# Expert weights in DRAM: from one matrix for each expert to blocks of two experts and 128 rows

## The chip, the cores and the metric

The kernel runs on one core of one Trainium2 chip. The metric is the device time of one execution in microseconds (us), the median of several executions.

## The reference, cut to what matters

Two layers follow each other. Each has a token mixer (two kinds of attention and a short convolution) and then a mixture of experts in which each of 16 experts picks 64 of the 512 tokens:

```
N_EXPERTS = 16; EXPERT_FF = 1024; D_MODEL = 1024      # all float32
x = x + einsum(mixed, w_out)                          # end of the mixer
xs   = x[idx]                                         # 64 tokens of each expert
hid  = silu(einsum('becd,edf->becf', xs, w_gate)) * einsum('becd,edf->becf', xs, w_up)
ys   = einsum('becf,efd->becd', hid, w_down) * gate
x    = x + zeros_like(x).at[bidx, idx].add(ys)
```

The three expert weights (`w_gate`, `w_up`, `w_down`) have the shape (2 layers, 16 experts, 1024, 1024), 4 MB for each expert and matrix. All 403 MB of them are read from device memory once per execution.

## The kernel before, in words

The tokens stay on the chip. A layer is `mixer()` and then `moe()`. The change touches `moe()` alone, and there only the loads of expert weights.

`moe()` works on 8 pairs of experts, one after the other. Both experts of a pair are multiplied at the same time: their 64 tokens each make the two column halves of TensorE's weights. For a pair the order is gate (8 chunks of 128 rows, contracted one after the other into the accumulators `G`), up (8 chunks, into `U`), activation and transposes, down (8 chunks, into `Y`), and then the scatter of the results to the token rows and the gather of the next pair's tokens. TensorE's matmuls run in exactly this program order (`PEo`).

A chunk is one call of `wload` (line 888): one transfer of 1 MB, 128 partitions by 2 experts by 1024 floats, into the next of 18 slots (`wslot`). All these loads are issued by SP, in program order, on one queue. SP issues a load when TensorE has read the chunk that was in its slot 18 loads earlier; each load also has one of eight semaphores in turn (DMAHW0 to DMAHW7 in the rows below), and waits for the load that had it before. `expert_mm` (line 915) takes a chunk with four matmuls (two halves of 512 columns by two experts), 8 instructions in the trace, since one float32 matmul is two instructions there.

The last pair's down projection is written apart (lines 1024 to 1036), because its two column halves `n` are finished one after the other: 16 transfers of 512 KB (line 1029), two for each step `kp` of 256 rows, each of pieces of 512 floats. After half `n` comes its scatter (`scatter_rows`), and in the last layer its output transfers. So the last loads of a layer stand directly ahead of its end.

`layouts()` runs on the host ahead of the kernel and arranges the inputs in device memory; it is not part of the time.

Of the kernel before, what the change touches and what calls it, by code (L numbers as in the profile page):

```python
# [18 lines left out]
L = 2  # L19
# [11 lines left out]
NE = 16  # L31
FF = 1024
CAP = 2 * S // NE
KC = D // 128
# [25 lines left out]
def token_of(j, p):  # L60
    return (p // CB) * GW + CB * j + p % CB


def constants():
    c = np.zeros((128, NCON), np.float32)
    c[:, _C["ident"][0]:_C["ident"][1]] = np.eye(128, dtype=np.float32)
    c[:, _C["iota"][0]:_C["iota"][1]] = np.arange(1, CAP + 1, dtype=np.float32)[None]
    c[:, _C["iotap"][0]] = (np.arange(128) % CAP + 1).astype(np.float32)
    inv = (np.float32(10000.0) ** (-np.arange(HALF, dtype=np.float32) / np.float32(HALF))).astype(np.float32)
    for j in range(NJ):  # L70
        t = token_of(j, np.arange(128)).astype(np.float32)
        ang = (t[:, None] * inv[None, :]).astype(np.float32).astype(np.float64)
        c[:, _C["cos"][0] + j * HALF:_C["cos"][0] + (j + 1) * HALF] = np.cos(ang)
        c[:, _C["sin"][0] + j * HALF:_C["sin"][0] + (j + 1) * HALF] = np.sin(ang)
    off = _C["mask"][0]
    for j, blocks in ((0, (0, 1)), (1, (0, 1, 2)), (3, (2, 3))):
        for b in blocks:
            q = CB * j + np.arange(128) % CB
            k = CB * b + np.arange(128) % CB
            st = np.clip(q - WW // 2, 0, GW - WW)[:, None]  # L80
            ok = (k[None] >= st) & (k[None] < st + WW)
            c[:, off:off + CB] = np.where(ok, 0.0, NEG)[:, :CB]
            off += CB
    c[:, _C["fold"][0]:_C["fold"][1]] = np.arange(128)[:, None] % 32 == np.arange(NE)[None, :]
    a, b = np.arange(128)[:, None], np.arange(128)[None, :]
    before = [a // CB < b // CB, a // CB == b // CB, (a // CB == b // CB) & (a < b)]
    return np.concatenate([c] + before, axis=1).astype(np.float32)
# [6 lines left out]
def build(tc, x_in, pp_in, con_in, gm_in, rpb_in, w_in, w_uq, w_ukv, w_out, w_gate, w_up, w_down, out,  # L94
# [3 lines left out]
    PE, ACT, DVE, POOL, SP = nc.tensor, nc.scalar, nc.vector, nc.gpsimd, nc.sync  # L98
# [6 lines left out]
    def tmp():  # L105
        return w2.tile([128, 512], F32, name="tmp", tag="tmp")

    def tmpr(name):
        return w2.tile([128, 512], F32R, name=name, tag="tmp")
# [700 lines left out]
    def moe(l, M, PSUM, pp, ctx2):  # L810
# [18 lines left out]
        for i in range(CAP // 8):  # L829
            src = work if i else p32[0:32, 0:256]  # L830
# [51 lines left out]
        def wslot():  # L882
            wi[0] += 1
            return wslots[(wi[0] - 1) % NSLOT]

        def wload(src, e0, k):
            t_ = wslot()
            SP.dma_start(t_, src[l, e0:e0 + 2, k * 128:(k + 1) * 128, :].rearrange("e p c -> p e c"))
            return t_

        def onehot(p):
# [75 lines left out]
        for p in range(NE // 2):  # L967
            e0 = 2 * p
            G = [acc(), acc()]
            if p:  # L970
                gate = gates(og2, e0)
                expert_mm(G, xs, w_gate, e0)
            else:
                gather(og2, 0, 1)
                for k in range(KC):
                    if k + 1 < KC:
                        gather(og2, k + 1, 1)
                    expert_mm(G, xs, w_gate, e0, range(k, k + 1))
                gate = gates(og2, e0)
                pt = wk()  # L980
                for j in range(NJ):
                    PEo.transpose(pt[0:NE, j * 128:(j + 1) * 128], slotn[:, j, :], ident)
                ACT.copy(slotT, pt[0:NE, :])
            if p < last:
                og2 = onehot(p + 1)
            U = [acc(), acc()]
            expert_mm(U, xs, w_up, e0)

            pb = wk()
            sel = st.tile([NE, 2, CAP], BF16, name="sel", tag="sel", bufs=2)  # L990
            POOL.tensor_copy(sel, ident[0:NE, e0:e0 + 2, None].to_broadcast([NE, 2, CAP]))  # L991
            PEo.matmul(pb, sel.rearrange("p e s -> p (e s)"), slotT, start=True, stop=True)
            hids = []
            for n in range(2):
                hid = tmp()
                ACT.activation(hid, G[n], AF.Silu)  # L996
                DVE.tensor_tensor(hid, U[n], hid, op=OP.mult)  # L997
                hids.append(hid)

            if p < last:  # L1000
                gather(og2, 0, 1)
            for n in range(2):
                pt = wk()
                for k in range(4):
                    PEo.transpose(pt[:, k * 128:(k + 1) * 128], hids[n][:, k * 128:(k + 1) * 128], ident)
                ACT.copy(hT[:, 4 * n:4 * n + 4, :], pt.rearrange("p (k s) -> p k s", k=4))  # L1006
            osc = tmpr("osc")
            DVE.tensor_scalar(osc, pb, C("iotap"), None, op0=OP.is_equal)
            Y = [acc(), acc()]
            if p < last:  # L1010
                gather(og2, 1, 1)
                expert_mm(Y, hs, w_down, e0)
                ys = [parts(Y, gate, 0), parts(Y, gate, 1)]
                gather(og2, 2)
                for s_ in range(4):
                    scatter(ys[s_], osc, s_)
                    if s_ < 2:
                        ys.append(parts(Y, gate, s_ + 2))
                    if s_ in (1, 2):
                        gather(og2, 2 * s_ + 2)  # L1020
                continue

            tc.keep_in_program_order(ACT.preload_act_table_set("natural_log_exp_and_others"))
            for n in range(2):
                for kp in range(KC // 2):
                    t_ = wslot() if l == layers - 1 else wslots[(4, 5, 0, 1, 2, 3)[(4 * n + kp) % 6]]
                    t_ = t_.rearrange("p a (b c) -> p a b c", b=2)
                    for e in range(2):
                        SP.dma_start(t_[:, :, e, :], w_down[l, e0 + e, kp * 256:(kp + 1) * 256, n * 512:(n + 1) * 512]
                                     .rearrange("(k p) c -> p k c", p=128))  # L1030
                    for kk in range(2):
                        k = 2 * kp + kk
                        for e in range(2):
                            PEo.matmul(Y[n][e * 64:(e + 1) * 64, :], hs(k, e), t_[:, kk, e, :], start=k == 0,
                                       stop=k == KC - 1)
                scatter_rows(Y, osc, gate, n)
# [6 lines left out]
def layouts(x, norm_mix, w_in, q_norm_a, k_norm_a, rpb, cq_norm, w_uq, ckv_norm, w_ukv, q_norm_b, k_norm_b,  # L1043
            conv_w, out_norm, w_out, norm_ffn, w_router, b_router, w_gate, w_up, w_down):

    def cols(a):
        return np.ascontiguousarray(a.reshape(-1, 128).T)

    pps = np.zeros((L, 128, NP), np.float32)
    for l in range(L):  # L1050
        def put(name, a):
            pps[l][:, _P[name][0]:_P[name][1]] = a
        put("gffn", cols(norm_ffn[l]))
        put("gout", cols(out_norm[l]))
        put("gqa", np.concatenate([q_norm_a[l]] * 2)[:, None])
        put("gka", np.concatenate([k_norm_a[l]] * 2)[:, None])
        put("gcq", cols(cq_norm[l]))
        put("gckv", cols(ckv_norm[l]))
        put("gqb", np.concatenate([q_norm_b[l, :DH], np.ones(DH, np.float32)])[:, None])
        put("gkb", np.concatenate([k_norm_b[l, :DH], np.ones(DH, np.float32)])[:, None])  # L1060
        put("convw", conv_w[l].reshape(3, 2, 128).transpose(2, 1, 0).reshape(128, 6))
        put("brt", np.broadcast_to(b_router[l], (128, NE)))
        put("gqr", np.broadcast_to(q_norm_b[l, DH:], (128, ROPE)))
        put("gkr", np.broadcast_to(k_norm_b[l, DH:], (128, ROPE)))
        put("wrt", w_router[l].reshape(KC, 128, NE).transpose(1, 0, 2).reshape(128, KC * NE))
    xp = x.reshape(8, NJ, CB, D).transpose(1, 0, 2, 3).reshape(NJ, 128, D)
    rp = np.pad(rpb, ((0, 0), (0, 0), (0, 0), (16, 16)))
    rp = np.stack([rp[..., 15 - c:63 - c] for c in range(CB)], axis=1).reshape(L, CB, NH, 15 * 48)
    return {"x": xp, "pp": pps, "con": constants(), "norm_mix": norm_mix, "rpb": rp, "w_in": w_in, "w_uq": w_uq, "w_ukv": w_ukv,
            "w_out": w_out, "w_gate": w_gate, "w_up": w_up, "w_down": w_down}  # L1070


_ORDER = ("x", "pp", "con", "norm_mix", "rpb", "w_in", "w_uq", "w_ukv", "w_out", "w_gate", "w_up", "w_down")
# [19 lines left out]
```

## Time and profile before

| | |
|---|---|
| median of 3 runs | 1555.66 us (1555.24 to 1555.86) |
| the profiled execution's own time | 1556.42 us |
| its span, first to last instruction | 1554.6 us |
| TensorE busy | 1484.8 us, 96% of the span |
| bytes read from device memory | 438.33 MB |
| transfers of 1 MB of expert weights | 368 (128 gate, 128 up, 112 down) |
| transfers of 512 KB of expert weights | 32 |

The profiled execution is 0.76 us above the median, and its span is 1.82 us shorter than its time. TensorE is busy nearly throughout, and from about 345 to 765 us and from about 1118 to 1540 us (the two `moe()` stages) the 16 DMA engines are busy throughout as well, so the page alone does not say which of the two sets the pace there.

### The profile page before, as it was taken

What the parts mean: (1) busy time and instruction counts of PE and PEld (TensorE: products, weight loads), DVE (VectorE), ACT (ScalarE), POOL (GpSimd) and SP (SyncE); (2) the same over time, 40 slices, a digit from 0 to 9 for tenths busy, and PEclk for the clock granted to TensorE, in tenths of its full rate; (3) what the DMA queues carried; (4) which work ended last, traced back from release to release, by engine and by line L of the source; (5) the groups of instructions that cost most, each with busy time, mean ns of one, the idle gap of its engine ahead of it and who ended that gap; (6) DMA issues with size and microseconds to landing.
All of it is one profiled execution on the core that took longest, in us unless ns stands there. A gap on an engine that the chain in (4) does not pass through costs nothing. (4 is left out here: it accounts for less than half of the span.)

```text
span 1554.6 us, 20383 instructions
## 1 busy us (share of the span) xinstructions
PE 1484.8 (96%) x8028; PEld 853.0 (55%) x8030; DVE 536.0 (34%) x1220; ACT 388.6 (25%) x969; POOL 232.2 (15%) x336
## 2 busy tenths in 40 slices
PE   7999999899999999899889999998999999999897
PEld 6877766645445534434278776665455355345342
DVE  5475456612122202212164644665122022122022
ACT  6465553300000000000164655542000000000001
POOL 4642350300000000000046314402000000000000
PEclk8999999999999999999999999999999999999999
DMA  5312123979999999999932112157999999999997
GB/s 168 87 45 68 48 82 124 362 286 410 409 409 409 409 409 409 409 409 409 354 100 71 49 54 74 56 218 285 370 409 409 409 409 409 409 409 409 409 409 283
DMA packets 138463, 441.76 MB, mean 284 GB/s; under 512 B 8832, under 2 KB 31360, under 8 KB 138368
## 3 DMA queue, kind: packets, MB, share of 16 engines
q1 hardware_dynamic: 136000, 437.06, 73.1%
q10 hardware_dynamic: 2368, 3.41, 0.7%
q8 instruction: 63, 1.03, 0.3%
q14 instruction: 32, 0.26, 0.0%
HBM read 438.33 MB, written 2.10 MB: 283 GB/s over the span
## 5 line engine op out<-in xcount | busy, mean ns | idle before, releaser
L158 PE MATMUL acc<-w,fmix 128*64 128x512 f32 x3072 | 684.7, 596 | 28.4 <-DMA w<-in_w_up_dram 14.9
L158 PEld LDWEIGHTS acc<-w,fmix 128*64 128x64 f32 x3072 | 213.8, 137 | 462.3 <-issue 377.8
L997 DVE TENSOR_TENSOR tmp<-acc,tmp 128x512 f32<-128x512 f32 x32 | 22.1, 691 | 410.8 <-issue 382.9
L158 PEld LDWEIGHTS wk<-og,fmix 128*128 128x128 f32 x1024 | 121.0, 192 | 25.9 <-issue 22.7
L158 PE MATMUL wk<-og,fmix 128*128 128x128 f32 x1024 | 132.2, 279 | 0.7 <-DVE og L893 0.7
L991 POOL CAST sel<-con 16x128 bf16<-16x128 f32 x16 | 4.9, 312 | 784.9 <-PE wk L158 778.6
L331 POOL TENSOR_TENSOR wring<-fraw,wring 128x384 fp32r<-128x384 f32 (+1 forms) x88 | 91.2, 1045 | 139.4 <-ACT wring L330 134.0
L996 ACT ACTIVATE tmp<-acc 128x512 f32<-128x512 f32 x32 | 18.9, 596 | 327.3 <-PE acc L158 327.3
L934 DVE SCALAR_TENSOR_TENSOR ys<-acc,stat,ys 128x256 fp32r<-128x256 f32 x56 | 26.8, 479 | 210.3 <-ACT ys L933 210.3
L933 ACT ACTIVATE ys<-acc,stat 128x256 fp32r<-128x256 f32 x56 | 26.5, 474 | 254.5 <-PE acc L158 203.3
L1006 ACT COPY fmix<-wk 128x512 f32<-128x512 f32 x32 | 17.4, 588 | 257.4 <-PE wk L161 257.4
L167 PE MATMUL prj<-wring,hn 128*128 128x384 f32 (+1 forms) x224 | 81.3, 363 | 0.2 <-DVE hn L310 0.2
L166 PE MATMUL prj<-wring,hn 128*128 128x384 f32 (+1 forms) x224 | 80.6, 361 | 0.4 <-ACT wring L330 0.4
L168 PE MATMUL prj<-wring,hn 128*128 128x384 f32 (+1 forms) x224 | 79.8, 356 | 0.1
L947 DVE TENSOR_TENSOR x<-wk,x 128x512 f32<-128x512 f32 x112 | 72.0, 684 | 2.2
L158 PE MATMUL wk<-ys,osc 128*128 128x256 f32 x448 | 63.8, 290 | 0.0
L903 DVE TENSOR_TENSOR fmix<-wk,pp 128x128 f32<-128x128 f32 (+1 forms) x86 | 30.6, 356 | 81.5 <-PE wk L158 81.5
L158 PEld LDWEIGHTS wk<-ys,osc 128*128 128x128 f32 x448 | 56.2, 191 | 0.0
L330 ACT CAST wring<-fraw 128x384 fp32r<-128x384 f32 (+1 forms) x88 | 44.4, 513 | 39.6 <-PE prj L167 15.6
L167 PEld LDWEIGHTS prj<-wring,hn 128*128 128x128 f32 x224 | 43.5, 194 | 5.6 <-issue 4.0
L168 PEld LDWEIGHTS prj<-wring,hn 128*128 128x128 f32 x224 | 43.3, 193 | 5.3 <-issue 3.7
L166 PEld LDWEIGHTS prj<-wring,hn 128*128 128x128 f32 x224 | 43.5, 194 | 4.8 <-issue 3.0
(272 smaller groups left out, 1992.7 us busy)
## 6 DMA issues: line engine op xcount, KB each, us to landing
w<-in_w_gate_dram SPq DMA_DIRECT2D x128, 1024.0 KB, 18.4
w<-in_w_up_dram SPq DMA_DIRECT2D x128, 1024.0 KB, 18.5
w<-in_w_down_dram SPq DMA_DIRECT2D x112, 1024.0 KB, 18.4
w<-in_w_down_dram SPq DMA_DIRECT2D x32, 512.0 KB, 10.8
fraw<-in_w_in_dram SPq DMA_DIRECT2D x24, 384.0 KB, 3.2
fraw<-in_w_out_dram SPq DMA_DIRECT2D x16, 512.0 KB, 3.5
fraw<-in_w_in_dram SPq DMA_DIRECT2D x48, 128.0 KB, 2.5
fmix<-in_rpb_dram ACTq DMA_DIRECT2D x16, 144.0 KB, 3.4
```

The costliest lines, as they stand in the source:

```text
L158: return tc.keep_in_program_order(PE.matmul(*a, **k))
L166: PE.matmul(ps, ah, bh, start=first, stop=False)
L167: PE.matmul(ps, al, bh, start=False, stop=False)
L168: PE.matmul(ps, ah, bl, start=False, stop=last)
L330: ACT.copy(hi, raw[:, kk, :])
L331: POOL.tensor_tensor(lo, raw[:, kk, :], f(hi), op=OP.subtract)
L903: DVE.tensor_tensor(xsT[:, k0:k0 + nk, :], pg[:, 0:nk * 128].rearrange("p (k s) -> p k s", k=nk), P("gffn")[:, k0:k0 + nk, None].to_broadc ...
L933: ACT.activation(ys[:, 0:256], yq, AF.Copy, scale=gate)
L934: DVE.scalar_tensor_tensor(ys[:, 256:512], yq, gate, f(ys[:, 0:256]), op0=OP.mult, op1=OP.subtract)
L947: DVE.tensor_tensor(xv, po.rearrange("p (j c) -> p j c", j=2), xv, op=OP.add)
L996: ACT.activation(hid, G[n], AF.Silu)
L997: DVE.tensor_tensor(hid, U[n], hid, op=OP.mult)
```

## The change

On the host, `layouts()` rearranges each expert matrix from (layer, expert, row, column) to (layer, pair, chunk of 128 rows, row in the chunk, expert of the pair, column). In device memory a chunk of a pair is then one contiguous block of 1 MB, and the 8 KB that one partition receives lie in one run; before, they were two runs of 4 KB, 4 MB apart.

`wload` reads that block as it lies. In the last pair's down projection the two transfers of a step are cut in another way: before, one transfer brought both chunks (`k`) of one expert; now one brings both experts of one chunk. Their pieces stay 512 floats (2 KB) long, and bytes and count of transfers stay what they were.

```
 def wload(src, e0, k):
     t_ = wslot()
-    SP.dma_start(t_, src[l, e0:e0 + 2, k * 128:(k + 1) * 128, :].rearrange("e p c -> p e c"))
+    SP.dma_start(t_, src[l, e0 // 2, k])
     return t_
...
     t_ = t_.rearrange("p a (b c) -> p a b c", b=2)
-    for e in range(2):
-        SP.dma_start(t_[:, :, e, :], w_down[l, e0 + e, kp * 256:(kp + 1) * 256, n * 512:(n + 1) * 512]
-                     .rearrange("(k p) c -> p k c", p=128))
+    for kk in range(2):
+        SP.dma_start(t_[:, kk], w_down[l, p, 2 * kp + kk, :, :, n * 512:(n + 1) * 512])
     for kk in range(2):
         k = 2 * kp + kk
         for e in range(2):
             PEo.matmul(Y[n][e * 64:(e + 1) * 64, :], hs(k, e), t_[:, kk, e, :], start=k == 0,
                        stop=k == KC - 1)
...
+def pairs(w):
+    return w.reshape(L, NE // 2, 2, KC, 128, FF).transpose(0, 1, 3, 4, 2, 5)
...
-        "w_out": w_out, "w_gate": w_gate, "w_up": w_up, "w_down": w_down}
+        "w_out": w_out, "w_gate": pairs(w_gate), "w_up": pairs(w_up),
+        "w_down": pairs(w_down)}
```

On SP, at the end of the last pair's up loads in the second layer, the queue before holds these rows (a row is a source line, a transfer with its target and source, and the shape of one transfer, partitions by elements):

```order
L888 DMA w_8277<-in_w_up_dram 128x2x1024
L888 DMA w_8278<-in_w_up_dram 128x2x1024
L1029 DMA w_8282<-in_w_down_dram 128x2x512 x2
L1029 DMA w_8283<-in_w_down_dram 128x2x512 x2
L1029 DMA w_8266<-in_w_down_dram 128x2x512 x2
```

The same place on SP with the change:

```order
L888 DMA w_8277<-in_w_up_dram 128x2048
L888 DMA w_8278<-in_w_up_dram 128x2048
L1029 DMA w_8282<-in_w_down_dram 128x2x512 x2
L1029 DMA w_8283<-in_w_down_dram 128x2x512 x2
L1029 DMA w_8266<-in_w_down_dram 128x2x512 x2
```

Order, slots and count of the transfers are the same; the loads of line 888 (368 of them) have become one run of 2048 floats for each partition, and the 512 KB transfers have the shape that they had.

On TensorE, the end of the second layer's last down projection (steps `kp` 2 and 3 of the second column half) stands so, with - for before and + for the change; the names in brackets are the semaphores of the transfers (DMAHW) that a matmul waits for:

```order
 L158 MATMUL acc<-w_8270,fmix 64x512 [waits DMAHW5_49]
+L158 MATMUL acc<-w_8270,fmix 64x512
 L158 MATMUL acc<-w_8270,fmix 64x512 [waits DMAHW0_49]
-L158 MATMUL acc<-w_8270,fmix 64x512 x2
+L158 MATMUL acc<-w_8270,fmix 64x512
 L158 MATMUL acc<-w_8271,fmix 64x512 [waits DMAHW2_49]
+L158 MATMUL acc<-w_8271,fmix 64x512
 L158 MATMUL acc<-w_8271,fmix 64x512 [waits DMAHW3_49]
-L158 MATMUL acc<-w_8271,fmix 64x512 x2
+L158 MATMUL acc<-w_8271,fmix 64x512
```

The second transfer of a step was waited for by the second of its four matmuls, and is now waited for by the third: two matmuls stand behind the last transfer of a half where three stood. The same holds in all 16 steps of the two layers, and nothing else moves on TensorE, VectorE, ScalarE or GpSimd.

## Rows read from the trace of the kernel before

**Rows 1.** The page: busy time of the engines; DMA in 40 slices.

```profile
PE 1484.8 (96%) x8028; PEld 853.0 (55%) x8030; DVE 536.0 (34%) x1220; ACT 388.6 (25%) x969; POOL 232.2 (15%) x336
...
GB/s 168 87 45 68 48 82 124 362 286 410 409 409 409 409 409 409 409 409 409 354 100 71 49 54 74 56 218 285 370 409 409 409 409 409 409 409 409 409 409 283
```

**Rows 2.** Stretches: busy us of each engine, clock, DMA share, GB/s.

```profile
345.00:750.00 405.00, 392.57 (x2155) 185.39 (x2153) 80.68 (x160) 29.06 (x56) 1.98 (x7) 1.00 1.03 408
1118.00:1521.00 403.00, 388.99 (x2137) 183.96 (x2133) 80.68 (x160) 29.07 (x56) 1.70 (x6) 1.00 1.03 409
1521.00:1530.00 9.00, 8.54 (x39) 3.47 (x40) 2.04 (x3) 2.46 (x3) 0.00 (x0) 1.00 1.05 387
```

**Rows 3.** What TensorE waited for: us in total, times, longest us.

```profile
PE acc L158 <- DMA w<-in_w_up_dram: 14.9, 24, 1.7
PE acc L158 <- DMA w<-in_w_down_dram: 12.9, 22, 0.7
```

**Rows 4.** Chain that ended last, second layer, in order of time: start, us, what.

```profile
1136.98 10.18 PE wk L158 x88
1147.15 27.62 PE acc L158 x128
...
1191.83 10.17 PE wk L158 x88
...
1301.51 10.17 PE wk L158 x88
...
1357.95 10.18 PE wk L158 x88
...
1419.33 10.18 PE wk L158 x88
...
1480.76 10.16 PE wk L158 x88
...
1532.12 1.95 PE acc L158 x6
...
1537.30 7.00 DMA w<-in_w_down_dram
1544.30 0.04 issue
1544.34 1.95 PE acc L158 x6
...
1550.86 0.60 DVEq L1088
```

**Rows 5.** Timeline of TensorE, last pair's up: start, us, instructions, idle before.

```profile
1512.46 1.94 PE L158 MATMUL acc<-w,fmix 128*64 128x512 f32 x8 [0.62 <-DMA w<-in_w_up_dram]
1515.02 1.94 PE L158 MATMUL acc<-w,fmix 128*64 128x512 f32 x8 [0.62 <-DMA w<-in_w_up_dram]
...
1521.28 1.94 PE L158 MATMUL acc<-w,fmix 128*64 128x512 f32 x8 [0.69 <-DMA w<-in_w_up_dram]
```

**Rows 6.** DMA packets, 1200 to 1500 us; the queue: packets, MB, share of 16 engines.

```profile
DMA packets 31780, 122.69 MB, mean 409 GB/s; under 512 B 1871, under 2 KB 1871, under 8 KB 31764
...
q1 hardware_dynamic: 31764, 122.45, 102.4%
```

**Rows 7.** The same, 1523 to 1531 us (512 KB transfers in flight).

```profile
DMA packets 1597, 3.07 MB, mean 384 GB/s; under 512 B 96, under 2 KB 96, under 8 KB 1597
...
q1 hardware_dynamic: 1597, 3.07, 104.5%
```

**Rows 8.** The same, 1236 to 1237.5 us.

```profile
q1 hardware_dynamic: 158, 0.60, 101.2%
q14 instruction: 1, 0.01, 1.3%
```

**Rows 9.** Timeline of SP: start, us, transfers issued.

```profile
1441.93 20.39 SPq L888 DMA_DIRECT2D w<-in_w_down_dram  x8
1462.41 20.35 SPq L888 DMA_DIRECT2D w<-in_w_gate_dram  x8
1482.86 18.41 SPq L888 DMA_DIRECT2D w<-in_w_up_dram  x7
```

**Rows 10.** The page: packets of the instruction queues, whole span.

```profile
q8 instruction: 63, 1.03, 0.3%
q14 instruction: 32, 0.26, 0.0%
```

## The prediction

> **What bounds the kernel now.** I read the page first: TensorE is 96% busy, and in the slices of both expert stages the DMA engines move 409 GB/s without a dip [rows 1]. Two resources are full at once, so the question is which one makes the other wait. The table of stretches puts numbers to it: from 345 to 750 us and from 1118 to 1521 us the DMA share is 1.03 at 408 and 409 GB/s, while TensorE idles for 12.4 and 14.0 us in them [rows 2]. TensorE's waits name the loads of up and down weights, 27.8 us over 46 waits [rows 3]. The chain of the second layer shows why so few. The same point of the work (the 88 instructions of scatter and gather) comes at 1136.98 and 1191.83 us: a pair takes TensorE 54.85 us. Later it comes at 1301.51, 1357.95, 1419.33 and 1480.76 us: 56.4, then 61.4 us for each pair [rows 4]. 24 loads of 1 MB (1,048,576 bytes) at 409 GB/s take 24 x 2.563 = 61.5 us. So TensorE starts a stage on slots loaded ahead, gains on the loads by 6.6 us with each pair, and from the fifth pair on goes at the pace of the loads: its chunks begin 2.56 us apart, 1.94 us of work and 0.62 us of wait [rows 5]. From about 345 and 1118 us to the last up load the transfer engines never stop, so what a transfer costs there comes back at the end of the stage, once for each transfer. SP is no limit: it issues one load after the other with no gap between them, at the pace at which they land (20.4 us for 8) [rows 9].
>
> **The 368 loads of 1 MB.** The change leaves the bytes and halves the pieces, if a run of 8 KB is moved as one packet. What does a packet cost besides its bytes? In the long stretch there are 31764 - 1871 = 29893 packets of 4 KB (122.4 MB) [rows 6]; behind the last up load, 2 KB packets alone (1501 of them, 3.07 MB) [rows 7] run at 387 GB/s [rows 2]. With 16 engines, a packet of 4096 B is spaced 4096 x 16 / 409 = 160.2 ns, one of 2048 B 2048 x 16 / 387 = 84.7 ns. A straight line through both gives 9.1 ns for a packet and 151.1 ns for 4 KB. A packet of 8 KB is then 9.1 + 302.2 = 311.3 ns, 1 MB (8 packets on each engine) 2.490 us instead of 2.563: 0.073 us less, or 421 GB/s. That is an extrapolation by one doubling. The records of the packets themselves give another price: 1.024 x 16 x 300 us / 29893 = 164 ns and 1.045 x 16 x 8 us / 1501 = 89 ns, so 2 x 89 - 164 = 14 ns a packet, and 0.11 us for a transfer. These records overlap (shares above 100%), so I take the spacing and keep 14 ns as a bound. The other bound is nothing.
>
> How many transfers count: 403 us / 2.563 = 157 in the second layer's stretch, 405 us at 408 GB/s likewise 157 in the first [rows 2]. Ahead of the stretch TensorE frees slots more slowly than they are filled, and there a faster transfer only waits. 157 x 0.073 = 11.5 us for each layer, 22.9 us in all. TensorE can take all of it: alone it would have ended the last up chunk at 1301.51 + 3 x 54.85 + 10.2 + 27.6 = 1503.9 us [rows 4], and it ended at 1521.28 + 1.94 = 1523.2 us [rows 5], so 19 us are there. With 24 x 2.490 = 59.8 us for a pair the loads still bind, and the waits remain, shorter and begun about a pair later.
>
> [...]
>
> **The 512 KB transfers at a layer's end.** Their pieces stay 2 KB, so their pace stays at 387 GB/s (1.355 us each); I cost the new addresses at nothing. But two matmuls now stand behind the last landing instead of three. Today 6 instructions take 1.95 us from the landing [rows 4], and 8 take 1.94 [rows 5], because a matmul for one expert alone takes as long as both experts side by side. Four instructions are one such pair less: a chunk in full flow is 27.62 us / 128 x 8 = 1.73 us [rows 4], half of that 0.86 us. At the layer's end this lies on the chain (landing at 1544.30, 6 instructions, scatter, output), so 0.86 us for each layer, 1.7 us in all. In the first column half the matmuls end earlier too, but the second half's last landing decides.
>
> **Other effects.** A packet of 8 KB holds an engine for 0.31 us instead of 0.16 us, so an instruction fetch on another queue can wait up to 0.15 us longer: 95 packets [rows 10], at most 14 us if each were waited for in full. TensorE's waits name no such thing today, so I cost it at nothing. The host's rearrangement lies outside the time.
>
> **Sum.** 22.9 + 1.7 = 24.6 us. The span of 1554.6 us becomes 1530.0 us; the median lies 1.06 us above the span, so 1531 us, or -1.6%.
>
> **Rivals.**
> *No wider packet, or no cost for each packet.* Nothing in the trace shows the weights' queue move a packet over 4 KB, so the 8 KB run may be cut at 4 KB. Or the fixed part belongs to the transfer, not the packet: both stretches have 16 packets on each engine for each transfer, so their rates alone cannot tell 9.1 ns a packet from 0.146 us a transfer. Then only 1.7 us come: 1554 us, within 0.2%. Against it: the recorded packets themselves are longer than in proportion (89 and 164 ns), and another queue does move packets of 8 KB (32 of 0.26 MB [rows 10]), one of them in 0.013 x 16 x 1.5 = 0.31 us beside the full load [rows 8]. [...]
> *Part of the gain.* The packet's price falls with its size, or instruction fetches take some back: 5 us for each layer instead of 11.5 gives 1544 us.
> *TensorE becomes the bound.* At 0.11 us a transfer the loads would give 157 x 0.11 = 17 us for each layer, near the 19 us that TensorE has: 1555.7 - 34 - 1.7 = 1520 us. Then a pair takes nearly 54.85 us throughout.
> *Slower.* All 16 engines now read side by side in one block of 1 MB, where each transfer spread over two blocks of 512 KB that lie 4 MB apart. If the memory serves that worse, every 1% of rate costs 314 x 0.0256 = 8.0 us, and nothing hides it, since the stretch has no slack. It shows as slower (over 0.2%, 3.1 us) from 1.7 + 3.1 = 4.8 us on, a transfer of 2.578 us. At the lowest rate that a stretch full of weights shows (387 GB/s, 2.71 us) it would be 157 x 0.147 = 23 us for each layer: 1600 us. For it: no row shows this pattern of addresses. Against: in the last pair, pieces of 2 KB out of every 4 KB run at a rate that packet size alone explains.
>
> **How the numbers follow.** A measurement of this kernel tells about 0.2% (3.1 us) from no change. Forecast (1524 to 1538 us) 0.60; part of the gain (1538 to 1552) 0.10; no gain from the packets 0.15; TensorE as the bound 0.02; slower 0.13. Faster is 0.60 + 0.10 + 0.02 = 0.72, same 0.15, slower 0.13. The range from 1523 to 1555 us leaves out the slower cases and the far end of the gain; the forecast's own range is 1524 to 1538.
>
> **What would show it.** Right: the weights' queue has about half the packets in the stretches (some 15 thousand of 8 KB in 300 us); some 421 GB/s; chunks 2.49 us apart where TensorE waits; late pairs 59.8 us; 4 instructions behind the last landing, about 1.1 us. Wrong: 409 GB/s with packets still at 4 KB (cut), or 409 GB/s with packets of 8 KB (the fixed part was the transfer's); a rate below 407 GB/s (addresses); or early pairs longer than 54.85 us, which would be a new wait that I do not see.

## The result, and the profile after

The changed kernel takes 1531.84 us (median of 4 runs, 1530.07 to 1532.34) against 1555.76 us: the ratio is 0.9844, 95% interval 0.9832 to 0.9857, so 23.9 us or 1.6% faster. The prediction was 1531 us. (A ratio is taken over executions at an undisturbed clock: one of the four of the run e4_two_transfers below took 2132.10 us at a granted clock of 0.915, against 0.964 to 0.972 in the others, so it counts in that run's median of 1958.27 us below and not in its ratio.) The profiled execution is the fastest of the four, 1530.07 us with a span of 1528.3 us, 26.3 us below the span of before.

The page of the changed kernel, the rows that answer to [rows 1], and the packets of the whole span (a packet is one piece of a transfer, as the profile records it):

```profile
PE 1478.7 (97%) x8030; PEld 855.0 (56%) x8030; DVE 537.0 (35%) x1220; ACT 388.8 (25%) x969; POOL 232.4 (15%) x336
...
GB/s 171 86 48 59 31 111 99 362 282 418 414 421 421 422 421 420 421 421 421 374 92 73 50 55 53 79 175 321 332 411 422 421 421 421 421 421 421 421 421 306
DMA packets 91359, 441.76 MB, mean 289 GB/s; under 512 B 8832, under 2 KB 31360, under 8 KB 44160
```

The same row of the kernel before:

```profile
DMA packets 138463, 441.76 MB, mean 284 GB/s; under 512 B 8832, under 2 KB 31360, under 8 KB 138368
```

The bytes are the same; the packets fell from some 138 thousand to 91 thousand, and the flat stretches stand at 421 GB/s instead of 409. The table of stretches (columns as in [rows 2]), nearly the same pieces of the program:

```profile
345.00:740.00 395.00, 390.39 (x2157) 186.65 (x2155) 80.70 (x160) 29.09 (x56) 1.99 (x7) 1.00 1.01 420
1100.00:1500.00 400.00, 395.55 (x2184) 188.72 (x2182) 82.72 (x163) 30.70 (x59) 1.70 (x6) 1.00 1.01 419
1500.00:1507.00 7.00, 6.34 (x30) 1.53 (x26) 0.00 (x0) 0.86 (x1) 0.00 (x0) 1.00 1.05 387
```

TensorE idles for 4.6 and 4.5 us in the two long stretches, where it idled for 12.4 and 14.0 us. The 2 KB packets behind the last up load (third row) run at 387 GB/s as before. TensorE's waits for weights, against the 27.8 us of [rows 3]:

```profile
PE acc L158 <- DMA w<-in_w_up_dram: 5.2, 10, 0.6
PE acc L158 <- DMA w<-in_w_down_dram: 4.9, 12, 0.6
```

The chain of the second layer now runs through loads alone late in the stage, so the pace of a pair is read from TensorE's timeline instead, at an instruction group that each pair has once (start, us):

```profile
1133.33 0.96 PE L158 MATMUL wk<-aff,og 128*128 128x16 f32 x8
...
1188.17 0.96 PE L158 MATMUL wk<-aff,og 128*128 128x16 f32 x8
...
1352.69 0.96 PE L158 MATMUL wk<-aff,og 128*128 128x16 f32 x8
...
1407.53 0.96 PE L158 MATMUL wk<-aff,og 128*128 128x16 f32 x8
...
1466.79 0.96 PE L158 MATMUL wk<-aff,og 128*128 128x16 f32 x8
```

A pair takes 54.84 us as long as the slots that were loaded ahead last, and 59.3 us in the one that waits. Before, the fifth pair was the first to slow down (56.4, then 61.4 us) [rows 4]; now it is the seventh. The chunks of the last up projection, which stand to [rows 5]:

```profile
1490.48 1.94 PE L158 MATMUL acc<-w,fmix 128*64 128x512 f32 x8 [0.26 <-DMA w<-in_w_up_dram]
1492.98 1.94 PE L158 MATMUL acc<-w,fmix 128*64 128x512 f32 x8 [0.56 <-DMA w<-in_w_up_dram]
1495.48 1.94 PE L158 MATMUL acc<-w,fmix 128*64 128x512 f32 x8 [0.57 <-DMA w<-in_w_up_dram]
```

They begin 2.50 us apart instead of 2.56, and the last one begins at 1495.48 us instead of 1521.28. The packets from 1200 to 1480 us, which answer to [rows 6]:

```profile
DMA packets 16175, 117.87 MB, mean 421 GB/s; under 512 B 1799, under 2 KB 1799, under 8 KB 1799
...
q1 hardware_dynamic: 16160, 117.65, 101.1%
```

16160 - 1799 = 14361 packets carry 117.6 MB: 8 KB each. The end of the chain in order of time (start, us, what):

```profile
1506.33 1.10 PE acc L158 x4
...
1509.53 3.35 PE wk L158 x7
1512.88 7.04 PE acc L158 x32
...
1522.08 2.60 PE wk L158 x7
```

Four instructions stand behind the first half's last landing, 1.10 us instead of 1.95.

### The profile page after: what moved, and what is told of

It reads as the page before. It is cut to its first block, busy times and chain, and to the rows that moved or that the text cites. A ratio compares the mean times of both kernels' runs of the same rounds, so it can differ in the third digit from the quotient of the medians.

```text
span 1528.3 us, 20385 instructions
## 1 busy us (share of the span) xinstructions
PE 1478.7 (97%) x8030; PEld 855.0 (56%) x8030; DVE 537.0 (35%) x1220; ACT 388.8 (25%) x969; POOL 232.4 (15%) x336
## 5 line engine op out<-in xcount | busy, mean ns | idle before, releaser
L158 PE MATMUL acc<-w,fmix 128*64 128x512 f32 x3072 | 675.2, 595 | 10.4 <-DMA w<-in_w_up_dram 5.2
```

The source lines that it names most:

```text
L158: return tc.keep_in_program_order(PE.matmul(*a, **k))
```

## The experiments

**Which part, and which property of it?** The change alters three things at once: the size of a packet, the addresses of a load (one block instead of two), and the cut of the last transfers. Three runs take them apart.

*Only the cut of the last transfers*, on the layout of before:

```
-for e in range(2):
-    SP.dma_start(t_[:, :, e, :], w_down[l, e0 + e, kp * 256:(kp + 1) * 256, n * 512:(n + 1) * 512]
-                 .rearrange("(k p) c -> p k c", p=128))
+for kk in range(2):
+    k = 2 * kp + kk
+    SP.dma_start(t_[:, kk], w_down[l, e0:e0 + 2, k * 128:(k + 1) * 128, n * 512:(n + 1) * 512]
+                 .rearrange("e p c -> p e c"))
```

> The old layout and the old 1 MB loads; only the last pair's 512 KB transfers are cut by chunk instead of by expert. Packet price (the theory of the prediction) and its rivals agree on the loads: 2.56 us for each, 409 GB/s, as before. The cut alone should bring 0.5 to 0.9 us for each layer (4 instructions behind the last landing instead of 6): 1554 to 1555 us, not to be told from before by the times; in the profile, from the last up load's landing to the end of the span 32.5 to 32.9 us instead of 33.4.

1555.23 us; ratio 0.9991, interval 0.9982 to 1.0000. The loads run as before (the stretch, then the queue from 1200 to 1480 us, of this kernel):

```profile
1118.00:1518.00 400.00, 387.88 (x2133) 183.63 (x2129) 80.70 (x160) 29.07 (x56) 1.70 (x6) 1.00 1.03 409
```

```profile
q1 hardware_dynamic: 29640, 114.28, 102.4%
```

Nearly all of the gain lies in the loads of line 888. What the cut brings is at the edge of what the times can tell, but TensorE's timeline shows it at the second layer's end (the last up chunk):

```profile
1521.13 1.94 PE L158 MATMUL acc<-w,fmix 128*64 128x512 f32 x8 [0.64 <-DMA w<-in_w_up_dram]
```

From the start of the last up chunk to the end of its span of 1554.0 us it took 32.9 us, within the 32.5 to 32.9 that were expected; before, it was 1554.6 - 1521.28 = 33.3 us [rows 5].

*The block of the change, but 4 KB packets*:

```
-    return w.reshape(L, NE // 2, 2, KC, 128, FF).transpose(0, 1, 3, 4, 2, 5)
+    w = w.reshape(L, NE // 2, 2, KC, 128, FF).transpose(0, 1, 3, 4, 2, 5)
+    return np.pad(w, ((0, 0),) * 5 + ((0, 64),))
...
-    SP.dma_start(t_, src[l, e0 // 2, k])
+    SP.dma_start(t_, src[l, e0 // 2, k, :, :, 0:FF])
```

> The changed kernel, but 256 B of padding stand behind each expert's 4 KB in device memory, so that the same block is read in packets of 4 KB; transfers, order and addresses are otherwise those of the change. Packet price: 16 packets on each engine again, 2.56 us a load, 409 GB/s, 1554 us. Rival, the addresses (one block instead of two that lie 4 MB apart) gave the gain: 2.49 us a load, about 1532 us.

1555.96 us; ratio 0.9997, interval 0.9988 to 1.0007. Its queue from 1200 to 1480 us:

```profile
DMA packets 29660, 114.51 MB, mean 409 GB/s; under 512 B 1743, under 2 KB 1743, under 8 KB 29645
```

409 GB/s: with 4 KB packets the block brings nothing.

*8 KB packets without a block* (a partition's runs 64 KB apart; the last transfers are read from the same layout):

```
-    return w.reshape(L, NE // 2, 2, KC, 128, FF).transpose(0, 1, 3, 4, 2, 5)
+    return w.reshape(L, NE // 2, 2, KC, 128, FF).transpose(0, 1, 4, 3, 2, 5)
...
-    SP.dma_start(t_, src[l, e0 // 2, k])
+    SP.dma_start(t_, src[l, e0 // 2, :, k])
...
-        SP.dma_start(t_[:, kk], w_down[l, p, 2 * kp + kk, :, :, n * 512:(n + 1) * 512])
+        SP.dma_start(t_[:, kk], w_down[l, p, :, 2 * kp + kk, :, n * 512:(n + 1) * 512])
```

> The changed kernel with packets of 8 KB, but a partition's runs lie 64 KB apart in device memory: no contiguous block for any load. Packet price: 2.49 us a load, about 421 GB/s, 1532 us, as with the change. Rival, the contiguous block gave the gain: at least 2.56 us a load, 1554 us or more.

1530.34 us; ratio 0.9834, interval 0.9817 to 0.9850. Its queue in the same stretch:

```profile
DMA packets 16174, 117.87 MB, mean 421 GB/s; under 512 B 1798, under 2 KB 1798, under 8 KB 1798
```

421 GB/s: the whole gain, from scattered addresses. At the addresses tried here the size of the run decides, not where the runs lie, and the theory of addresses falls on both sides.

**Is the price one for each packet, or one for each transfer?** The first attempt doubled the transfers of the changed kernel by halves of the partitions:

```
-    SP.dma_start(t_, src[l, e0 // 2, k])
+    for h in range(2):
+        SP.dma_start(t_[h * 64:(h + 1) * 64], src[l, e0 // 2, k, h * 64:(h + 1) * 64])
```

> The changed kernel, but each 1 MB load is two transfers of 64 partitions; packets stay at 8 KB and their number is the same, the number of transfers doubles. Packet price: 2.49 to 2.51 us for 1 MB, 1532 to 1537 us. Rival, the fixed part (0.146 us) belongs to each transfer: 2.63 us for 1 MB, which is 157 x 0.146 = 23 us more for each layer, about 1577 us.

1958.27 us; ratio 1.257, interval 1.2546 to 1.2595: slower than either theory said. Its queue from 1500 to 1700 us:

```profile
DMA packets 9517, 62.44 MB, mean 312 GB/s; under 512 B 1902, under 2 KB 1902, under 8 KB 1902
...
q1 hardware_dynamic: 9509, 62.32, 101.8%
```

9509 - 1902 = 7607 packets of 8 KB take 1.018 x 16 x 200 us / 7607 = 428 ns each, where the changed kernel has 1.011 x 16 x 280 / 14361 = 315 ns. The rate is not the same throughout: in the two stages the slices of its page go from 219 to 323 GB/s.

```profile
GB/s 154 65 54 58 66 160 220 224 282 297 293 295 309 308 306 282 307 316 308 290 57 52 62 63 50 219 230 274 294 302 320 323 312 310 284 243 238 244 295 259
```

The packets themselves have become longer, so this run does not answer the question that it was made for. The next one doubles the transfers over all 128 partitions, on the kernel before:

```
-    SP.dma_start(t_, src[l, e0:e0 + 2, k * 128:(k + 1) * 128, :].rearrange("e p c -> p e c"))
+    for e in range(2):
+        SP.dma_start(t_[:, e], src[l, e0 + e, k * 128:(k + 1) * 128, :])
```

> The kernel before, but each 1 MB load is two transfers of 512 KB over all 128 partitions, one for each expert: packets stay at 4 KB, their number is the same, the number of transfers doubles. Packet price: 2.56 us for 1 MB plus one more completion packet on each engine (the few-byte packets, some 0.01 us), 1555 to 1560 us. Rival, the fixed part (0.146 us) belongs to each transfer: 2.71 us for 1 MB, 157 x 0.146 = 23 us more for each layer, about 1602 us.

1554.46 us; ratio 0.9983, interval 0.9974 to 0.9992. The queue from 1200 to 1480 us:

```profile
DMA packets 31402, 114.50 MB, mean 409 GB/s; under 512 B 3488, under 2 KB 3488, under 8 KB 31387
...
q1 hardware_dynamic: 31387, 114.29, 102.5%
```

Twice the few-byte packets (3488), the same 409 GB/s. A transfer has no price that shows here; the price belongs to the packet. The run is even 2.7 us faster than the kernel before beside it (1557.16 us), just below the 1555 to 1560 that were expected; where that comes from was not followed up.

**Why was the split by halves so slow?**

```
-    SP.dma_start(t_, src[l, e0 // 2, k])
+    for h in range(2):
+        SP.dma_start(t_[h:128:2], src[l, e0 // 2, k, h:128:2])
```

> As e4_two_transfers (two transfers of 64 partitions for 1 MB, packets of 8 KB), but the transfers take the even and the odd partitions instead of the lower and the upper half. Theory for the slow e4: 16 engines that write into 64 neighbouring partitions get in each other's way at the on-chip memory (packets of 468 ns instead of 312 in e4); alternate partitions spread over all of it, so packets of about 312 ns, 2.5 us for 1 MB, 1532 to 1540 us. Rival, a transfer over 64 partitions is slow by itself: as e4, about 1958 us.

1532.34 us; ratio 0.9842, interval 0.9826 to 0.9859. Its queue from 1200 to 1480 us:

```profile
DMA packets 17958, 117.83 MB, mean 421 GB/s; under 512 B 3588, under 2 KB 3588, under 8 KB 3588
...
q1 hardware_dynamic: 17942, 117.60, 101.1%
```

Also two transfers of 64 partitions for 1 MB, and as fast as one: 1.011 x 16 x 280 / (17942 - 3588) = 316 ns a packet. (The 468 ns of the expectation are the spacing at a rate of 280 GB/s, 8192 x 16 / 280; the recorded length in the window shown is 428 ns.) So it is the choice of 64 neighbouring partitions that stretches packets, 428 ns against 316. The two runs differ in the source addresses as well, but e5_by_expert reads contiguous blocks of 512 KB, as the run by halves does, without a loss (409 GB/s, as the kernel before). That engines get in each other's way at the on-chip memory is the author's theory; the runs show the lengths of the packets, not what lies behind them.

**Does the line go on?** Two chunks in one transfer, runs of 16 KB, 9 slots of 2 MB (left out: the order of the slots, and the halves of slots that the first layer's last transfers get):

```
-    wslots[i] = M.tile([128, 2, FF], F32, name=f"w{i}", tag=f"w{i}")
+    wslots[i] = M.tile([128, 2, 2, FF], F32, name=f"w{i}", tag=f"w{i}")
...
+    if k % 2 == 0:
+        wcur[0] = wslot()
+        SP.dma_start(wcur[0], src[l, e0 // 2, k // 2])
+    return wcur[0][:, k % 2]
...
+    return w.reshape(L, NE // 2, 2, KC // 2, 2, 128, FF).transpose(0, 1, 3, 5, 4, 2, 6)
```

> The changed kernel with two chunks in one transfer: 2 MB, a run of 16 KB for each partition, 9 slots of 2 MB instead of 18 of 1 MB. Packet price on the same line: 9.1 + 604.4 = 613.5 ns a packet, 2.454 us for 1 MB, 427 GB/s, 157 x 0.031 = 4.9 us less for each layer; the coarser slots are freed one chunk later, which costs about 2 us for each layer: about 1526 us (1523 to 1530). Rival, a packet ends at 8 KB or has a price that grows with its size: 2.49 us for 1 MB, 1532 to 1537 us.

1531.06 us (1527.51 to 1532.57); ratio 0.9832, interval 0.9814 to 0.9849. Its queue from 1200 to 1480 us, the stretch behind the first layer's up loads, and what SP waited for there (us in total, times, longest us):

```profile
DMA packets 8211, 119.62 MB, mean 427 GB/s; under 512 B 909, under 2 KB 909, under 8 KB 909
```

```profile
735.00:755.00 20.00, 15.71 (x69) 5.52 (x67) 5.08 (x9) 3.40 (x5) 0.28 (x1) 1.00 0.96 339
```

```profile
SPq L1036 <- DMA w<-in_w_up_dram: 29.2, 3, 24.1
```

The rate is the one on the line, 427 GB/s, but the time is hardly below the change's and misses the expected 1523 to 1530 us. The last loads of the first layer (the stretch) run with gaps at 339 GB/s: they had been given slots that the last up loads still held, and SP waited up to 24.1 us for one of these.

*Runs of 4 KB in the last down projection*, on the changed kernel (left out: the load of line 1029, which reads the new blocks as they lie):

```
+    last = w_down[:, NE - 2:].reshape(L, 2, KC, 128, 2, 512).transpose(0, 4, 2, 3, 1, 5)
+    down[:, -1] = last.reshape(down[:, -1].shape)
```

> The changed kernel with the last pair's down weights laid out by column half, so that its 512 KB transfers have runs of 4 KB instead of 2 KB. Packet price: 1.28 us for each 512 KB instead of 1.355 (16 packets of 4 KB on each engine for 1 MB), so the first half's last landing comes 8 x 0.075 = 0.6 us earlier after the last up load; up to 1.2 us for each layer, 1529.5 to 1531.5 us, hardly to be told by the times, but by the landings in the trace. Rival, these loads are bound by the semaphores or the memory and not by their packets: still 1.355 us.

1531.17 us; ratio 0.9834, interval 0.9819 to 0.9848. The stretch behind its last up load:

```profile
1498.00:1506.00 8.00, 7.95 (x41) 2.81 (x37) 2.04 (x3) 2.45 (x3) 0.00 (x0) 1.00 1.03 410
```

410 GB/s where the change has 387: these loads follow their packets too. The landings show it as well, at the last up chunk of the second layer and at the matmuls behind the first half's last landing:

```profile
1497.48 1.94 PE L158 MATMUL acc<-w,fmix 128*64 128x512 f32 x8 [1.08 <-DMA w<-in_w_up_dram]
1507.73 1.08 PE L158 MATMUL acc<-w,fmix 128*64 128x512 f32 x4 [0.20 <-DMA w<-in_w_down_dram]
```

They lie 10.25 us apart, where the change has 1506.33 - 1495.48 = 10.85: the 0.6 us that were expected. The time does not tell it from the change, as was expected.

**A faster version.** The two runs that followed gave the 2 MB slots other places in memory, so that the first layer's last transfers find free slots; the second also has the 4 KB runs at the end. The changed kernel ran beside them.

```
-    for i in (2, 3, 4, 6, 7, 0, 5, 8, 1):
+    for i in (5, 6, 7, 8, 1, 2, 3, 4, 0):
...
+    t_ = wslots[(2, 3, 4, 0)[i_ // 2]][:, i_ % 2]
```

> As e6_16k (2 MB transfers, runs of 16 KB), with other slots for the first layer's last down projection. In e6_16k the last up load of the first layer landed 4.5 us earlier than with the change, but the next layer began no earlier, since the tail's first transfers waited for the slot of the last up load. Theory: with slots that are free by then the 4.5 us come through, 1531.1 - 4.5 = 1526.5 us (1525 to 1528). Rival, something else binds the first layer's end (TensorE, or the mixer's memory): 1530 to 1532 us.

> e10_16k_slots and e7_tail_4k together: 2 MB transfers with runs of 16 KB, and runs of 4 KB in the last pair's down projection. Packet price: 0.6 to 1.2 us for each layer less than e10_16k_slots, 1524 to 1526 us. Rival, the tail is TensorE's by now: as e10_16k_slots.

> The changed kernel itself beside the two others, for a comparison on one chip: 1530 to 1533 us.

1546.57 us (ratio 0.9937, interval 0.9921 to 0.9952), 1548.00 us (0.9945, 0.9932 to 0.9958) and 1532.45 us (0.9849, 0.9832 to 0.9866). Both theories for the slots were wrong. SP's timeline of the first of them, as the mixer of the second layer ends (start, us, transfers), and a wait of SP there:

```profile
1027.78 34.29 SPq L889 DMA_DIRECT2D w<-in_w_gate_dram  x4
1062.17 2.69 SPq L889 DMA_DIRECT2D w<-in_w_up_dram  x4
```

```profile
SPq L889 <- PE prj L168: 32.5, 1, 32.5
```

The first four loads took 34 us to issue and the next four followed within 3 us: the second load's slot stood in memory that the mixer used nearly to its end (SP waited 32.5 us for a matmul of the mixer), and SP, which issues in order, held all others behind it. The stage began with fewer slots filled: from 1010 to 1090 us the DMA engines moved 176 GB/s, where e6_16k has 297. The last run changes the places once more:

```
-    for i in (5, 6, 7, 8, 1, 2, 3, 4, 0):
+    for i in (1, 4, 5, 7, 8, 2, 3, 6, 0):
...
-    t_ = wslots[(2, 3, 4, 0)[i_ // 2]][:, i_ % 2]
+    t_ = wslots[(2, 3, 0, 2)[i_ // 2]][:, i_ % 2]
```

> As e8_16k_tail_4k, but the nine slots stand in memory so that the first four loads of a stage go where the mixer's buffers are released first (in e10_16k_slots the second load of each stage waited 33 us for its slot, and SP, which issues in order, held all others behind it), and the first layer's last transfers go to slots that are free by then. Theory: the prefetch is whole again and the wider packets come through, 1524 to 1527 us. Rival, the 2 MB slots cost as much as the packets bring (coarser release): 1530 to 1532 us, as e6_16k.

1523.38 us (1522.46 to 1526.26); ratio 0.9799, interval 0.9784 to 0.9814, which lies wholly below that of the change. Two stretches, and TensorE's waits for weights, of this kernel:

```profile
345.00:735.00 390.00, 387.52 (x2151) 186.75 (x2147) 80.70 (x160) 29.07 (x56) 1.98 (x7) 1.00 1.01 426
735.00:755.00 20.00, 17.14 (x79) 6.53 (x79) 5.49 (x9) 3.40 (x5) 0.28 (x1) 1.00 0.99 395
```

```profile
PE acc L158 <- DMA w<-in_w_down_dram: 5.0, 4, 1.4
PE acc L158 <- DMA w<-in_w_up_dram: 2.7, 3, 1.2
```

The tail of the first layer is full again (395 GB/s where e6_16k has 339), the long stretch is at 426 GB/s, and TensorE waits for weights 7.7 us in all. The run holds three things at once (runs of 16 KB, the places of the slots, runs of 4 KB at the end), and their shares were not taken apart.

## Why the prediction was right

*The bound.* It said that a late pair goes at the pace of the loads and that their time comes back at the end of the stage. It did: the chunks moved from 2.56 to 2.50 us apart, and the last up chunk of the second layer came 25.8 us earlier.

*The packet's price.* From 2 KB and 4 KB packets the line gave 9.1 ns a packet and 421 GB/s for 8 KB. Measured are 421 GB/s, and for 16 KB 427 GB/s, that is 16384 x 16 / 427 = 614 ns where the line has 613.5. That this is a price of the packet, not of the transfer, the place or the layout, was argued ahead and is now shown by three runs: 4 KB packets from the same block give no gain (409 GB/s), 8 KB packets from scattered runs give it all (421 GB/s), and twice the transfers cost nothing (409 GB/s). The recorded lengths, by which a packet would cost 14 ns, overstated it. The sum chose the 387 GB/s of [rows 2] for 2 KB packets; with the 384 of [rows 7] the same line gives 10.4 ns a packet and 423 GB/s, so the exact hit on 421 is in part that choice.

*How much of it reaches the end.* 22.9 us were counted for the loads. The last up chunk's 25.8 us hold that of both layers, the first layer's tail, and whatever else differs between two executions; the medians differ by 23.9 us, of which the cut of the last transfers has part. In the first layer alone, where 11.5 us were counted, the last up chunk came 752.36 - 739.15 = 13.2 us earlier in this pair of executions, and 11.9 to 12.7 us earlier in the traces of after_again, e3_pitch_64k, e7_tail_4k and e9_alternate. So the term was, if anything, a little small; it agrees with the medians within what the runs scatter. One statement was off without a cost: the waits were to begin about a pair later, and began two pairs later.

*The last transfers.* 0.86 us for each layer were counted, at the second half's last landing. The matmuls behind a last landing did shrink from 1.95 to 1.10 us, but neither layer went the way that the prediction gave.

In the first layer the size was right and the path was not. The last up chunk and the second column half, the kernel before (two rows) and then the changed one (two rows):

```profile
752.36 1.94 PE L158 MATMUL acc<-w,fmix 128*64 128x512 f32 x8 [0.61 <-DMA w<-in_w_up_dram]
769.05 7.09 PE L158 MATMUL acc<-w,fmix 128*64 128x512 f32 x32
739.15 1.94 PE L158 MATMUL acc<-w,fmix 128*64 128x512 f32 x8 [0.59 <-DMA w<-in_w_up_dram]
754.97 7.09 PE L158 MATMUL acc<-w,fmix 128*64 128x512 f32 x32
```

In both kernels the second half's 32 instructions run through without a wait, so there its landings decide nothing. What decides is the first half's last landing, which the prediction set aside. From the last up chunk to the second half it took 16.69 us and takes 15.82, 0.87 us less. That the number fits is luck: the cut happens to take the same two instructions from either half.

In the second layer the second half's last landing did decide before (it is on the chain in [rows 4]), but less came of it: from the start of the last up chunk to the end of the span it took 1554.6 - 1521.28 = 33.3 us before and 1528.3 - 1495.48 = 32.8 us after, 0.5 us less. The scatter between the halves took longer: its last 7 instructions 3.35 us, against 1.9 us before (from 1536.15 to 1538.06 us). In that stretch the granted clock was 0.57 (0.50 from 1509.5 to 1512.5 us) and the scatter's matmuls came 0.43 us apart; the same place of before has 1.00, and 0.23 us. First the changed kernel, then the kernel before:

```profile
1509.00:1513.00 4.00, 3.97 (x10) 2.52 (x12) 2.63 (x5) 0.00 (x0) 0.00 (x0) 0.57 0.94 332
```

```profile
1535.50:1538.00 2.50, 2.35 (x10) 1.43 (x10) 1.79 (x4) 0.08 (x1) 0.00 (x0) 1.00 0.79 271
```

So the second half began late, found its weights landed, and ran through without a wait (7.04 us): its end was TensorE's and not the landing's. In e3_pitch_64k, which has the same cut, the path is the one predicted:

```profile
1498.35 1.94 PE L158 MATMUL acc<-w,fmix 128*64 128x512 f32 x8 [0.45 <-DMA w<-in_w_up_dram]
1521.42 1.08 PE L158 MATMUL acc<-w,fmix 128*64 128x512 f32 x4 [0.99 <-DMA w<-in_w_down_dram]
```

Its second half waits for its last landing, and the matmuls end 1521.42 + 1.08 - 1498.35 = 24.15 us after the start of the last up chunk, against 1544.34 + 1.95 - 1521.28 = 25.01 us before [rows 4]: the 0.86 us. There the clock fell in the scatter behind them (0.65, the first row below), and 0.5 us are left at the end of the span (1531.2 - 1498.35 = 32.85 us, against 33.32 before).

The scatters are the same work in all these kernels, so I put their extra time to the clock. Its fall does not come with the change. Three scatters of the second layer, in order e3_pitch_64k (behind the halves), e1_tail_only (between them, loads as before) and e5_by_expert (behind them, loads cut in two and the last transfers as before):

```profile
1524.00:1528.00 4.00, 3.45 (x8) 1.99 (x8) 2.90 (x5) 0.11 (x1) 0.00 (x0) 0.65 0.29 109
1534.00:1538.00 4.00, 3.33 (x8) 2.13 (x8) 2.48 (x5) 0.47 (x1) 0.00 (x0) 0.69 0.84 301
1545.00:1549.00 4.00, 3.29 (x8) 1.88 (x8) 2.95 (x5) 0.11 (x1) 0.00 (x0) 0.67 0.31 114
```

TensorE had idled 1.60 us just before the scatter in e1_tail_only, 1.6 us on average in e5_by_expert (6.4 us in 4 waits), and 1.59 and 1.65 us in the kernel before too, where the clock stayed at 1.00; why it fell in some and not in others stays open.

*The costs put at nothing.* Instruction fetches beside longer packets: no wait of TensorE names one, and the sum closes without them. Addresses: e3_pitch_64k (421 GB/s with 8 KB packets) and e2_gap_4k (409 with 4 KB) show no effect of either sign, which answers the rival that the block is served worse.

*The rivals.* A cut at 4 KB is refuted by the packets of 8 KB, and a part of the gain (1544 us) by the full 421 GB/s in both stages; TensorE did not become the bound, since 10 us of waits for weights remain.

## What to carry to other kernels

Where a stretch is bound by transfers, look at the size of their packets before their number or their addresses: here two rates at two packet sizes in one trace (387 GB/s at 2 KB, 409 at 4 KB) gave a line, and it foretold the rate at two and four times the size (421 and 427 GB/s). A saving for each transfer was counted for as many transfers as lie in the stretch that has no slack (157 in each layer, an estimate from 403 us at 2.563 us each), and only up to what the waiting engine could take (19 us, an estimate from 54.85 us a pair). Wider runs needed wider slots, and where these stood in memory cost more than the packets brought (1546.57 us in e10_16k_slots, 1532.45 us for the change beside it): a prefetch in issue order was held by the first slot that was not free, for 32.5 us.

## What the runs showed of the hardware

The weights' queue moved runs of 8 and 16 KB as single packets, which no row of before showed, at 421 and 427 GB/s beside 409 for 4 KB and 387 for 2 KB. In e6_16k 8211 - 909 = 7302 packets carry 119.6 MB, 16 KB each.

Two transfers of 64 neighbouring partitions ran at 312 GB/s with packets of 428 ns in the window shown (e4_two_transfers), two of 64 alternate partitions at 421 GB/s with 316 ns (e9_alternate). Why the packets of neighbouring partitions are longer was not measured.
